# A ring of weight units made six deep instead of five, fetched five ahead, in a one-core decoder layer

## The chip, the cores and the metric

The kernel runs on one core of one Trainium2 chip. Its time is the device time of the core in microseconds; before the change the median of 3 runs is 420.98 us (420.36 to 421.74). The engines are TensorE (PE, matrix products), VectorE (DVE), ScalarE (ACT), GpSimd (POOL) and SyncE (SP), which here issues nearly all loads.

## The reference: what is computed

One layer of a decoder on 256 tokens of width 1024, in float32:

```python
proj = x @ w_in                       # all queries, keys, values of three mixers
o_a, o_b, o_c = sparse_attention(...), dilated_attention(...), block_attention(...)
gates = sigmoid(x @ w_gate)           # 3 x 1024 columns
merged = gates[0]*(o_a @ w_br_a) + gates[1]*(o_b @ w_br_b) + gates[2]*(o_c @ w_br_c)
x = layer_norm(ALPHA * x + merged @ w_out)
h = square(relu(x @ w_up)) @ w_down   # 1024 -> 4096 -> 1024
ple = sigmoid(x @ w_ple_gate) * (p @ w_ple)
x = layer_norm(ALPHA * x + h + ple)
```

A table of relative-position biases (one column per head) is added to all attention logits.

## The kernel before

**Products in three parts.** Each float32 product is made of three products of a shorter float type: every factor is split into a high part (a cast) and a low part (what the cast lost), and `prod` (L184, the matmul is L189) adds high x high, high x low and low x high in PSUM. The input `x` is split once into `xh` and `xl`. The weights come from memory and have to be split as they come.

**The ring of weights.** The class `Weights` (L80) keeps a list of units, in the order in which the program will use them; a unit is up to 128 x 1024 numbers (512 KB). `_split` handles one: SP loads it into a tile of the ring `raw` (L103), ACT casts it into a tile `whi` of the ring `part` (L110 or L112), and DVE subtracts the cast from the raw tile into `wlo` (L119 or L123); for the first 58 units POOL does the last columns of that. A raw tile is free again when the cast and the subtraction have read it; `whi` and `wlo` when TensorE has used them. `get(i, ahead)` (L128) hands out unit i, and before that makes sure that the units up to i + `ahead` have had their `_split` written into the program. `ahead` is `AHEAD` unless a caller gives another number: the steps of the wide products (L642, L651), their ends (`min(AHEAD, ...)`, L662 and L1044).

**What sets the order.** Each engine runs its instructions in a fixed order. It is not the order of the code: a scheduler that goes through the program with a simulated timeline places each instruction (L1158), and what has been written earlier goes first among those that are ready in that simulation. So a number like `AHEAD` can move instructions anywhere. SP's queue holds all loads of weights, the tiles `T` of the bias table (L265), the loads of `xr` (below) and the stores of the result; one that waits holds up those behind it.

**The stages.** (1) Until 17 us: first loads, split of `x`, first products. (2) Until 188.7 us the mixed part: the attention of the three mixers, with the products for their queries, keys and values, the gates (`fill("g")`) and the second and third branch (`fill("c")`, L335 to L348) put in between. `V` is cleared out of PSUM by L399, the keys by L318. (3) The merges: `merge(p)` for p = 0 to 3 (L675) multiplies the first branch by its weights (`w_br_a`), then DVE adds the gate (two L688, from PSUM into `G`), adds the other branches (L689), ACT writes the high half of two merged rows (two L693) and DVE the low half (two L694) into the tile `store`. (4) The out projection: `outp.step(k)` for k = 0 to 3 and then `finish` multiply the merged rows by the eight units of `w_out`, here called w0 to w7 (merged row k with w_k, four groups of three products; in each step the eight products with the high half of the row come first, then the four with the low half). The parts of w0 to w3 lie in the ring, those of w4 to w7 in the tile `store`, so in the orders below a split of w4 to w7 reads `store<-raw`. (5) First layer norm, the small branch `ple` and its gate, until 247 us. (6) The up projection until 330.5 us: 32 units, each 16 matmuls (L918, L921). (7) The down projection until 412 us. Pairs of its units go through a Strassen scheme: SP loads a pair into `xr` (L871, L873), DVE forms sums of its blocks (`form`, L880 to L882), and four tiles are split instead of two. (8) The second layer norm and the output, until 418.6 us.

Of the kernel before, what the change touches and what calls it, by code (L numbers as in the profile page):

```python
# [35 lines left out]
AQ, AK, AV, IQ, IK, IW, BQ, BK, BV, CQ, CK, CV = (  # L36
    0, 384, 448, 512, 1024, 1088, 1096, 1864, 2120, 2376, 2760, 3144)

AHEAD = 4
FIRST = 4  # L40
DV = 640

# [37 lines left out]
class Weights:  # L80
# [46 lines left out]

    def get(self, i, ahead=AHEAD):  # L128
        while self.done <= min(i + ahead, len(self.units) - 1):
            with ExitStack() as held:  # L130
                held.enter_context(self.tc.high_priority(offset=self.units[self.done][6]))
                ins = self.after
                if self.units[self.done][2] is not None:

                    ins = (*ins, self.copies[-1], self.subs[-1])
                for x in ins:
                    held.enter_context(self.tc.issue_after(x))
                self._split(self.done)
            self.done += 1
        return self.parts.pop(i)  # L140
# [3 lines left out]
def hybrid_layer(ctx: ExitStack, tc: tile.TileContext, x0, xn, pT, wqk, wva, wvb, wg, wbc, wba,  # L144
                 wout, wup, wdn, wpg, wple, lnrow, rel, onehot, pick, out):
    nc = tc.nc
    pe, act, dve, pool = nc.tensor, nc.scalar, nc.vector, nc.gpsimd

    keep = ctx.enter_context(tc.tile_pool(name="keep", bufs=1))
    raw = ctx.enter_context(tc.tile_pool(name="raw", bufs=5))  # L150
    part = ctx.enter_context(tc.tile_pool(name="part", bufs=5))
    queries = ctx.enter_context(ExitStack())
    qpool = queries.enter_context(tc.tile_pool(name="q", bufs=8))
    dram = ctx.enter_context(tc.tile_pool(name="dr", bufs=1, space=DRAM))
# [479 lines left out]
    class Wide:  # L634
# [6 lines left out]

        def get(self, k, ahead=AHEAD):  # L642
            if k not in self.ws:
                self.ws[k] = W.get(self.units[k], ahead)
# [5 lines left out]

        def step(self, k, ahead=AHEAD, bs=(0, 1), last=None, whole=None):  # L651

            self.get(k, ahead)
            for b in bs:
                for c, cs in enumerate(H):
                    end = (whole or len(self.units)) if cs in self.cut[b] else last
                    self.go(self.acc[b][c], k, b, cs, 0, end - 1)

        def finish(self, ks, done, spare):

            for k in ks:
                self.ws[k] = W.get(self.units[k], min(AHEAD, ks[-1] - k + spare))  # L662
            for b in range(2):
# [379 lines left out]
    X = p2.tile([128, 2, D], F32, name="X", tag="X")  # L1043
    ws = {k: W.get(u_dn[k][0], min(AHEAD, 31 - k)) for k in LATE}  # L1044
    accs = (P[4], P[8]), (P[2], *ends)
# [116 lines left out]
```

## Time and profile before

| | us |
|---|---|
| median of 3 runs | 420.98 |
| profiled execution | 420.38 |
| span in the profile | 418.6 |
| TensorE busy | 405.4 (97%) |
| DVE busy | 350.7 (84%) |
| ACT busy | 277.4 (66%) |
| POOL busy | 120.5 (29%) |

The profile is of one execution; 1.8 us of it lie outside the span. The granted clock of TensorE is 0.996 of full speed. A wait that the profile lists as "A <- B" is time in which engine A stood still, and B is what ended it.

### The profile page before, as it was taken

What the parts mean: (1) busy time and instruction counts of PE and PEld (TensorE: products, weight loads), DVE (VectorE), ACT (ScalarE), POOL (GpSimd) and SP (SyncE); (2) the same over time, 40 slices, a digit from 0 to 9 for tenths busy, and PEclk for the clock granted to TensorE, in tenths of its full rate; (3) what the DMA queues carried; (4) which work ended last, traced back from release to release, by engine and by line L of the source; (5) the groups of instructions that cost most, each with busy time, mean ns of one, the idle gap of its engine ahead of it and who ended that gap; (6) DMA issues with size and microseconds to landing.
All of it is one profiled execution on the core that took longest, in us unless ns stands there. A gap on an engine that the chain in (4) does not pass through costs nothing.

```text
span 418.6 us, 7824 instructions
## 1 busy us (share of the span) xinstructions
PE 405.4 (97%) x2804; PEld 373.6 (89%) x2804; DVE 350.7 (84%) x650; ACT 277.4 (66%) x530; POOL 120.5 (29%) x128
## 2 busy tenths in 40 slices
PE   7999999999999999999999999999999999999993
PEld 7988999999999999999787889999999988788883
DVE  4969668978778679889977889999999788999856
ACT  5878366396798885866606567887789766467320
POOL 1579456254354558500000002432430000000001
PEclk9999999999999999999999999999999999999998
DMA  8795977567465407479790686786576277555602
GB/s 282 279 325 171 258 255 204 151 205 275 129 216 159 133 0 262 144 223 333 246 329 0 203 299 199 223 284 201 177 221 207 91 279 236 173 176 198 205 2 101
DMA packets 28300, 84.30 MB, mean 201 GB/s; under 512 B 2992, under 2 KB 7128, under 8 KB 27876
## 3 DMA queue, kind: packets, MB, share of 16 engines
q1 hardware_dynamic: 26880, 79.41, 58.7%
q10 hardware_dynamic: 1284, 4.32, 3.0%
q8 instruction: 22, 0.36, 0.4%
q14 instruction: 18, 0.15, 0.1%
q0 software_dynamic: 96, 0.06, 0.0%
HBM read 81.88 MB, written 1.90 MB: 200 GB/s over the span
## 4 chain that ended last, share of the span: by engine, by line
PE 66%; DVE 15%; DMA 10%; issue 4%; ACT 2%; POOL 1%; SPq 1%; DVEq 0%; ACTq 0%; POOLq 0%
PE mm L189 26%; PE mm L918 13%; PE b L189 12%; PE mm L921 7%; DVE wlo L119 6%; PE b L368 2%; DMA xr<-in_wdn_dram 2%; DMA raw<-in_wqk_dram 2%; DMA raw<-in_wout_dram 2%; PE b L514 2%; DVE wlo L123 2%; DMA G<-in_x_dram 1%; ACT whi L112 1%; PE b L410 1%; DMA raw<-in_wg_dram 1%
## 5 line engine op out<-in xcount | busy, mean ns | idle before, releaser
L112 ACT CAST whi<-raw 128x1024 fp32r<-128x1024 f32 (+3 forms) x92 | 89.7, 986 | 39.1 <-PE b L189 14.3
L123 DVE TENSOR_TENSOR wlo<-raw,whi 128x256 fp32r<-128x256 f32 (+3 forms) x118 | 96.7, 843 | 16.8 <-ACT whi L112 13.6
L189 PE MATMUL mm<-xh,whi 128*128 128x256 f32 x336 | 89.2, 278 | 0.0
L123 POOL TENSOR_TENSOR wlo<-raw,whi 128x384 fp32r<-128x384 f32 (+1 forms) x50 | 68.1, 1371 | 69.6 <-ACT whi L112 68.2
L189 PE MATMUL mm<-xl,whi 128*128 128x256 f32 x336 | 86.9, 276 | 0.0
L189 PE MATMUL mm<-xh,wlo 128*128 128x256 f32 x336 | 79.9, 279 | 1.3 <-DVE k L318 0.8
L189 PEld LDWEIGHTS mm<-xh,whi 128*128 128x128 f32 x336 | 64.4, 192 | 0.9
L189 PEld LDWEIGHTS mm<-xl,whi 128*128 128x128 f32 x336 | 64.5, 192 | 0.1
L918 PE MATMUL mm<-x,whi 128*128 128x512 f32 x256 | 60.7, 379 | 0.0
L189 PEld LDWEIGHTS mm<-xh,wlo 128*128 128x128 f32 x336 | 58.8, 192 | 2.1 <-PE mm L189 0.9
L189 PE MATMUL b<-whi,store 128*128 128x512 f32 x168 | 52.6, 380 | 1.0 <-DVE store L694 0.7
L918 PEld LDWEIGHTS mm<-x,whi 128*128 128x128 f32 x256 | 46.1, 190 | 5.2
L119 DVE TENSOR_TENSOR wlo<-raw,whi 128x1024 fp32r<-128x1024 f32 (+2 forms) x38 | 42.9, 1153 | 3.3 <-ACT whi L112 3.1
L735 POOL TENSOR_TENSOR rs<-rs,half 128x1 f32<-128x1 f32 x4 | 2.7, 664 | 142.2 <-DVE rs L734 142.2
L110 ACT CAST whi<-raw 128x256 fp32r<-128x256 f32 x64 | 36.4, 612 | 6.1 <-PE b L189 3.7
L189 PEld LDWEIGHTS b<-whi,store 128*128 128x128 f32 x168 | 31.7, 189 | 6.0 <-DVE store L694 1.1
L921 PEld LDWEIGHTS mm<-x,wlo 128*128 128x128 f32 x256 | 33.6, 191 | 1.7
L921 PE MATMUL mm<-x,wlo 128*128 128x256 f32 x256 | 33.7, 275 | 0.0
L189 PE MATMUL b<-wlo,store 128*128 128x512 f32 x84 | 32.1, 382 | 0.7 <-DVE wlo L119 0.6
L942 POOL TENSOR_TENSOR a<-a 128x128 f32<-128x128 f32 x7 | 7.3, 1044 | 58.4 <-ACT a L904 52.8
L189 PE MATMUL mm<-op,whi 128*128 128x256 f32 x128 | 22.1, 278 | 0.0
L189 PE MATMUL b<-whi,x 128*128 128x512 f32 x64 | 19.8, 384 | 0.1
(223 smaller groups left out, 822.5 us busy)
## 6 DMA issues: line engine op xcount, KB each, us to landing
raw<-in_wup_dram SPq DMA_DIRECT2D x32, 512.0 KB
raw<-in_wg_dram SPq DMA_DIRECT2D x24, 512.0 KB
raw<-in_wqk_dram SPq DMA_DIRECT2D x18, 512.0 KB
raw<-in_wdn_dram SPq DMA_DIRECT2D x18, 512.0 KB
raw<-in_wout_dram SPq DMA_DIRECT2D x8, 512.0 KB
raw<-in_wpg_dram SPq DMA_DIRECT2D x8, 512.0 KB
T<-tabd SPq DMA_DIRECT2D x24, 128.0 KB
xr<-in_wdn_dram SPq DMA_DIRECT2D x6, 512.0 KB
```

The lines of the kernel that those rows point to most:

```text
L110: i = nc.scalar.copy(blocks(hi, a, b), blocks(r, a, b))
L112: i = nc.scalar.copy(hi, r)
L119: i = e.tensor_tensor(lo[:, x], r[:, x], hi[:, x].bitcast(F32), op=ALU.subtract)
L123: i = e.tensor_tensor(blocks(lo, *x), blocks(r, *x), blocks(hi, *x).bitcast(F32), op=ALU.subtract)
L189: i = pe.matmul(ps, lhsT=a[x], rhs=b[y], start=first and n == 0, stop=last and n == 2, skip_group_check=more)
L368: m = pe.matmul(ss[2 * n + h][:, QC[b]], lhsT=q[d, x, c], rhs=k[d, y, 0:128 * (b + 1)], start=i == 0, stop=i == 2)
L410: pe.transpose(t[:, 128 * i:128 * i + 128], P[:, 128 * i:128 * i + 128], ident)
L514: pe.matmul(pairs(first[f]), lhsT=w[:, k, 128 * f:128 * f + 128], rhs=inturn(x[:, k]), start=k == i == 0, stop=k == KT - 1 and i == 2)
L735: pool.tensor_tensor(rs, rs, half, op=ALU.pow)
L918: pe.matmul(ps, lhsT=hi[:, c], rhs=x1[:, :, k].rearrange("p b a t -> p a t b"), start=k == 0, stop=False)
L921: pe.matmul(ps[:, 0], lhsT=lo[:, c], rhs=x1[:, :, k, 0].rearrange("p b t -> p t b"), start=False, stop=k == KT - 1)
L942: pool.tensor_tensor(sums[2], a11, a21, op=ALU.subtract)
```

## The change

`AHEAD` goes from 4 to 5, the rings `raw` and `part` get six tiles each instead of five, and the argument `dynamic_dma_scratch_size=2048` shrinks the memory that is set aside in SBUF for transfers whose descriptors are written by POOL. There are three such transfers, all at the start (the bias table's inputs, L479 to L481). The freed memory is 14336 bytes per partition, and the ring needs 13312 more (4096 for a `raw` tile, 4352 for `whi`, 4864 for `wlo`).

```diff
--- before.py
+++ after.py
@@ -36,7 +36,7 @@
 AQ, AK, AV, IQ, IK, IW, BQ, BK, BV, CQ, CK, CV = (
     0, 384, 448, 512, 1024, 1088, 1096, 1864, 2120, 2376, 2760, 3144)
 
-AHEAD = 4
+AHEAD = 5
 FIRST = 4
 DV = 640
 
@@ -147,8 +147,8 @@
     pe, act, dve, pool = nc.tensor, nc.scalar, nc.vector, nc.gpsimd
 
     keep = ctx.enter_context(tc.tile_pool(name="keep", bufs=1))
-    raw = ctx.enter_context(tc.tile_pool(name="raw", bufs=5))
-    part = ctx.enter_context(tc.tile_pool(name="part", bufs=5))
+    raw = ctx.enter_context(tc.tile_pool(name="raw", bufs=6))
+    part = ctx.enter_context(tc.tile_pool(name="part", bufs=6))
     queries = ctx.enter_context(ExitStack())
     qpool = queries.enter_context(tc.tile_pool(name="q", bufs=8))
     dram = ctx.enter_context(tc.tile_pool(name="dr", bufs=1, space=DRAM))
@@ -1149,7 +1149,8 @@
     from concourse.bass_utils import run_bass_kernel_spmd
 
     laid = _layout(**{n: np.asarray(a) for n, a in inputs.items()})
-    nc = bacc.Bacc("TRN2", target_bir_lowering=False, num_devices=1)
+    nc = bacc.Bacc("TRN2", target_bir_lowering=False, num_devices=1,
+                   dynamic_dma_scratch_size=2048)
     arrays, args = {}, []
     for n, a in laid.items():
         arrays[f"in_{n}_dram"] = a
```

No instruction is added or taken away. What moves is their order. Three places follow, each before and after; "x2" is a row that comes twice in a row.

DVE in the merges, from the split of w1 or w2 (`wlo<-raw,whi`, of the out projection) to the first or second pair of L694. Before:

```order
L119 TENSOR_TENSOR wlo<-raw,whi 128x1024
L689 TENSOR_TENSOR G<-G 128x2x256
L688 SCALAR_TENSOR_TENSOR G<-G,mm 128x256 x2
L119 TENSOR_TENSOR wlo<-raw,whi 128x1024
L688 SCALAR_TENSOR_TENSOR G<-G,mm 128x256 x2
L694 SCALAR_TENSOR_TENSOR store<-G,store 128x256
L689 TENSOR_TENSOR G<-G 128x2x256
L694 SCALAR_TENSOR_TENSOR store<-G,store 128x256
L119 TENSOR_TENSOR wlo<-raw,whi 128x1024
L688 SCALAR_TENSOR_TENSOR G<-G,mm 128x256 x2
L689 TENSOR_TENSOR G<-G 128x2x256
L119 TENSOR_TENSOR store<-raw,store 128x1024 x3
```

After:

```order
L119 TENSOR_TENSOR wlo<-raw,whi 128x1024
L348 TENSOR_TENSOR G<-G,mm 128x256
L689 TENSOR_TENSOR G<-G 128x2x256
L688 SCALAR_TENSOR_TENSOR G<-G,mm 128x256 x2
L119 TENSOR_TENSOR wlo<-raw,whi 128x1024
L119 TENSOR_TENSOR store<-raw,store 128x1024
L688 SCALAR_TENSOR_TENSOR G<-G,mm 128x256 x2
L689 TENSOR_TENSOR G<-G 128x2x256
L119 TENSOR_TENSOR store<-raw,store 128x1024 x2
L688 SCALAR_TENSOR_TENSOR G<-G,mm 128x256 x2
L694 SCALAR_TENSOR_TENSOR store<-G,store 128x256 x2
L119 TENSOR_TENSOR store<-raw,store 128x1024
```

Before, the first L694 follows the split of w2, and w3 and the first three store units come between it and the second pair. After, the split of w3 and those of w4, w5 and w6 are ahead of the first L694, and only one store unit is left behind it.

ACT at the same place, from the load of the residual `X` (L719, on ACT's queue) to the first pairs of L693. Before:

```order
L719 DMA X<-in_xn_dram 128x2048
L112 CAST whi<-raw 128x768
L112 CAST whi<-raw 128x1024 x3
L693 ACTIVATE store<-G 128x256 x2
L112 CAST whi<-raw 128x1024
L112 CAST store<-raw 128x1024 x3
L693 ACTIVATE store<-G 128x256 x2
L112 CAST store<-raw 128x1024
```

After:

```order
L719 DMA X<-in_xn_dram 128x2048
L112 CAST whi<-raw 128x1024 x4
L112 CAST store<-raw 128x1024 x3
L693 ACTIVATE store<-G 128x256 x2
L112 CAST store<-raw 128x1024
L112 CAST whi<-raw 128x1024
L693 ACTIVATE store<-G 128x256 x2
L112 CAST whi<-raw 128x1024
L693 ACTIVATE store<-G 128x256 x2
```

Before, the first pair of L693 follows three casts of 1024 columns (w0 to w2). After, it follows seven: w0 to w3, and w4 to w6 into `store`.

SP where the down projection begins, with its loads `raw` (single units) and `xr` (pairs). Before:

```order
L103 DMA raw<-in_wup_dram 128x1024 x12
L103 DMA raw<-in_wdn_dram 128x1024 x5
L871 DMA xr<-in_wdn_dram 128x1024
L873 DMA xr<-in_wdn_dram 128x512 x2
L871 DMA xr<-in_wdn_dram 128x1024
L873 DMA xr<-in_wdn_dram 128x512 x2
```

After:

```order
L103 DMA raw<-in_wup_dram 128x1024 x11
L103 DMA raw<-in_wdn_dram 128x1024 x7
L871 DMA xr<-in_wdn_dram 128x1024
L873 DMA xr<-in_wdn_dram 128x512 x2
L871 DMA xr<-in_wdn_dram 128x1024
L873 DMA xr<-in_wdn_dram 128x512 x2
```

Seven loads into the ring stand ahead of the first `xr` where five stood, and one follows the second pair where two did.

## The prediction

> **What bounds the kernel now.** I read the head of the page first, then TensorE's waits, then the same busy times by stretch.
>
> ```profile
> span 418.6 us, 7824 instructions
> PE 405.4 (97%) x2804; PEld 373.6 (89%) x2804; DVE 350.7 (84%) x650; ACT 277.4 (66%) x530; POOL 120.5 (29%) x128
> q0 software_dynamic: 96, 0.06, 0.0%
> PE b L180 <- POOL ident masks.py:199: 1.7, 1, 1.7
> PE mm L189 <- DVE k L318: 0.8, 1, 0.8
> PE b L514 <- ACT sh L507: 0.7, 1, 0.7
> PE b L189 <- DVE store L694: 0.7, 1, 0.7
> PE b L189 <- DVE wlo L119: 0.7, 2, 0.6
> PE mm L189 <- DVE V L399: 0.6, 1, 0.6
> PE mm L189 <- DVE wlo L123: 0.4, 1, 0.4
> PE b L189 <- DVE b L992: 0.3, 1, 0.3
> SPq L103 <- DVE wlo L123: 142.5, 72, 13.4
> SPq L265 <- DMA tabd<-tab: 9.0, 1, 9.0
> ```
>
> TensorE is the bound: 97% of the span, and its waits (in us: total, times, longest) add up to 5.9. A deeper ring can act on those for weights or for what stands behind a split: the two split rows (0.7 and 0.4), the V row (0.6), and perhaps the store row (0.7). That is 2.4 us, 0.6%, the most that can be won unless an order changes elsewhere. The large number, 142.5 us of SP waiting for a ring slot, is cover and not cost: SP issues nothing else that is due then.
>
> ```profile
> 80.00:188.70 108.70, 107.65 (x936) 104.60 (x935) 86.56 (x216) 82.57 (x186) 52.42 (x46) 1.00 0.56 175
> 188.70:212.00 23.30, 22.56 (x140) 20.44 (x140) 23.06 (x37) 14.87 (x20) 0.00 (x0) 1.00 0.84 287
> 247.00:330.50 83.50, 83.50 (x512) 76.68 (x511) 80.40 (x126) 70.04 (x149) 21.49 (x28) 1.00 0.66 204
> 330.50:412.00 81.50, 80.04 (x383) 68.56 (x381) 70.75 (x83) 41.46 (x47) 0.55 (x1) 1.00 0.54 179
> ```
>
> These are stretches (from:to, length; PE, PEld, DVE, ACT, POOL busy with counts; clock, DMA share, GB/s). One stretch stands out: from 188.7 to 212 (the merges and the out projection) DVE is busy 23.06 of 23.30 us. There DVE has no slack, so the order in which its work stands decides when TensorE may go on. In the up projection (247 to 330.5) TensorE is busy throughout and waits for nothing.
>
> **The change, part by part. The merges** carry the largest term. With one more unit allowed ahead, the splits of w3 and of the store units w4, w5, w6 now stand ahead of the merged rows on both DVE and ACT. What the trace of before has there (start, duration, engine, operation, idle and releaser):
>
> ```profile
> 188.75 0.95 DVE L123 TENSOR_TENSOR wlo<-raw,whi 128x768 fp32r<-128x768 f32 x1
> 195.13 1.22 DVE L119 TENSOR_TENSOR wlo<-raw,whi 128x1024 fp32r<-128x1024 f32 x1 [0.24 <-ACT whi L112]
> 196.27 0.74 DVE L688 SCALAR_TENSOR_TENSOR G<-G,mm 128x256 f32<-128x256 f32 x2
> 196.93 0.42 DVE L694 SCALAR_TENSOR_TENSOR store<-G,store 128x256 fp32r<-128x256 f32 x1
> 197.27 0.68 DVE L689 TENSOR_TENSOR G<-G 128x512 f32<-128x512 f32 x1
> 200.60 3.49 DVE L119 TENSOR_TENSOR store<-raw,store 128x1024 fp32r<-128x1024 f32 x3
> 204.01 0.75 DVE L694 SCALAR_TENSOR_TENSOR store<-G,store 128x256 fp32r<-128x256 f32 x2
> ```
> ```profile
> 195.00 0.71 ACT L693 ACTIVATE store<-G 128x256 fp32r<-128x256 f32 x2
> 197.76 1.04 ACT L112 CAST store<-raw 128x1024 fp32r<-128x1024 f32 x1 [0.16 <-DMA raw<-in_wout_dram]
> ```
> ```profile
> 196.67 0.38 PE L189 MATMUL b<-whi,store 128*128 128x512 f32 x1
> 198.40 1.24 PE L189 MATMUL b<-whi,store 128*128 128x512 f32 x5
> 204.48 1.35 PE L189 MATMUL b<-whi,store 128*128 128x512 f32 x5 [0.74 <-DVE store L694]
> ```
>
> Step 0 of the out projection starts at 196.67 with the high half of merged row 0 (L693). At 198.40 come its products with the low half, which DVE had started to write at 196.93 (L694). Start to start a split takes 1.14 us (195.13 to 196.27), a pair of L688 0.66 (196.27 to 196.93), an L689 0.60 (197.27 to 197.87, where the next L694 starts; by its record 0.68).
>
> In the changed order four splits (4 x 1.14 = 4.56), one L688 pair (0.66) and one L689 (0.60) move ahead of the first L694: 5.82 us. Against that, DVE enters the stretch one split richer (the 768-wide one at 188.75, 0.86 start to start), and the 0.24 us of idle time at 195.13 goes, since w2's load is issued a slot earlier. So L694 starts 5.82 - 0.86 - 0.24 = 4.72 us later, at 201.65, and its first row is there at 202.0. Step 0's low products start then instead of at 198.40: 3.6 us late.
>
> ACT is not what ends last. If the load of w6 takes the place in time that w5 had, its cast starts at 197.76, takes 1.04, and L693 follows at about 198.8. TensorE then starts step 0 near 199.2, does eight products until 200.9, and waits for DVE until 202.0. If w6's load came no earlier than before, about one cast later, the eight products would end at about 202.1, the same point within 0.1.
>
> Part of the lag comes back at once. Before, TensorE stood for 0.74 us at 204.48, because three splits were ahead of the second pair of L694 on DVE. After, step 2's low products are due at about 207.2, and the L694 that they need follows the first pair by two splits and an L689: 201.65 + 0.75 + 2 x 1.14 + 0.60 = 205.3. That stall is gone. Net 3.6 - 0.74 = **+2.9 us**. Upper end +4 (a cast or the wait for a load comes on top, 1.04, with a little more). Lower end +0.5, if DVE got two more splits (2.3 us) done before 188.7. What stands behind it, LN1's statistics and then the gates and the up projection, is late by the same amount, and by the row of 247 to 330.5 TensorE has no idle time there to make it up.
>
> **The mixed attention** (until 188.7) has weights at two stalls:
>
> ```profile
> 92.33 1.24 DVE L123 TENSOR_TENSOR wlo<-raw,whi 128x640 fp32r<-128x640 f32 x1 [0.31 <-ACT whi L112]
> 93.49 1.01 DVE L399 TENSOR_TENSOR V<-mm,V 128x384 fp32r<-128x384 f32 x2
> 94.09 0.38 PE L189 MATMUL mm<-xh,wlo 128*128 128x256 f32 x1 [0.56 <-DVE V L399]
> 156.34 0.49 PE L189 MATMUL mm<-op,wlo 128*128 128x256 f32 x2 [0.39 <-DVE wlo L123]
> ```
>
> At 94.09 TensorE waits for a PSUM bank that L399 clears, and L399 stands behind the split at 92.33. In the changed order a split more has been done by then, so L399 can start about 1.16 us sooner (92.33 to 93.49) and the whole 0.56 goes. At 156.34 the unit's own split is late by 0.39; with a unit more in stock it should not be. Together 0.95, and I take **-1.0**. The lower end is -2.0, twice that, for small gaps that the waits don't list. The upper end comes from SP: three more raw loads now stand ahead of the first bias tiles (T, L265), 512 KB each and 3.0 us at the 175 GB/s of the row of 80 to 188.7, 9.0 us in all. SP's queue already stands 9.0 us for the bias table at that place, which covers them; if half of one load sticks out, the bias tiles and the softmax behind them are 1.5 late, so +1.5.
>
> **The down projection** (330.5 to 412) is where DVE has to split the loaded weights and form the Strassen sums.
>
> ```profile
> 330.70 0.33 SPq L871 DMA_DIRECT2D xr<-in_wdn_dram  x1
> 333.27 1.23 DVE L119 TENSOR_TENSOR wlo<-raw,whi 128x1024 fp32r<-128x1024 f32 x1 [0.74 <-ACT whi L112]
> 335.62 1.23 DVE L880 TENSOR_TENSOR rows<-xr 128x1024 f32<-128x1024 f32 x1 [0.79 <-DMA xr<-in_wdn_dram]
> 337.30 1.23 DVE L119 TENSOR_TENSOR wlo<-xr,whi 128x1024 fp32r<-128x1024 f32 x1 [0.46 <-ACT whi L112]
> 340.22 0.81 PE L189 MATMUL b<-whi,PL 128*128 128x512 f32 x3
> 356.28 1.23 DVE L880 TENSOR_TENSOR Y<-xr 128x1024 f32<-128x1024 f32 x1 [1.58 <-DMA xr<-in_wdn_dram]
> ```
>
> DVE stands idle 0.74 + 0.79 + 0.46 + 1.58 = 3.57 us here for casts and loads, and TensorE waits for splits 0.7 us in all (the row of waits above, two times; 81.50 - 80.04 = 1.46 us of every kind). In the changed order the splits of units 2 and 3 come a turn earlier, inside the up projection, where DVE has 83.5 - 80.4 = 3.1 us to spare. That fills the idle 0.74 and perhaps some of the rest. Against it, the first xr load stands behind seven raw loads instead of five. It waits for the last reader of x1 until 330.70 in any case. The seventh raw load needs the slot that unit 2's split frees at about 330, so its 512 KB (2.9 us at 179 GB/s) may be on the queue when xr is issued. TensorE needs the first split of the pair at 340.22 and has it at 338.5, 1.7 us early; a delay of up to 1.7 is covered, 1.2 more is not. I take **-0.7**, the waits for splits, since the filled 0.74 is as large; the ends are -1.5 (all of TensorE's idle time) and +1.2.
>
> The Trainium skill speaks against this part ("DMA: Bandwidth & Descriptors", Queues, rings and completion order): on each DMA engine descriptors are consumed in ring order, so what SP issues first goes first. By that the whole seventh load would lie ahead of xr. No row of before shows seven loads ahead of it.
>
> **The rest at 0**: LN1 and the ple gate get one more cast between turns of ACT, which is busy 66%; ends -0.5 and +0.5. The shrunken memory for dynamic transfers serves q0 alone, with 96 packets and 0.06 MB; 0 unless its three transfers now wait for each other, which I bound by one landing of the longest of them, 5.6 us:
>
> ```profile
> DMA to landing us min/median/max: 5.6/5.6/5.6
> ```
>
> Only the bias table hangs on them, and that this decides is less than 1 in 20. The Trainium skill ("DMA: Bandwidth & Descriptors", Terms) says that such transfers have their 16-byte descriptors written to rings in SBUF. With one or two descriptors a packet, 96 packets would be 1.5 or 3 KB, an estimate on either side of the new size; no run here shows what it costs.
>
> **Sum**: +2.9 - 1.0 - 0.7 + 0 = +1.2 us. The profiled execution took 420.38 us (span 418.6 and 1.8 around it), 0.6 under the median of 420.98. 420.38 + 1.2 = 421.6; on the scale of the median **422.2**, a shade slower.
>
> **Rivals.** *Slower, the longer queue*: the merges cost the full 2.9, the mixed stage gains nothing as T comes late behind the three loads, and xr comes 1.2 later than its cover: 2.9 + 0 + 1.2 = +4.1, 425.1. For it: T and xr share SP's queue with the ring, and DVE waits for xr even now. Against it: the cover of 1.7 us. It decides from a delay of xr above 1.7 us. *Faster, the stock pays*: the mixed stage reaches its lower end (-2.0), the down stage -1.0, and in the merges DVE comes two splits richer, so that the lag shrinks to 0.5: -2.5, 418.5. For it: the waits exist, and DVE has idle time before 188.7 (86.56 busy of 108.70). Against it: four splits stand ahead of L694 and the merges have none. *Nothing*: the ring fills off TensorE's path and DVE comes in time everywhere, 421.0. For it: 97% busy. Against it: the new order on DVE in a stretch without slack.
>
> **How the numbers follow.** The forecast has 0.45, the slower rival 0.18, the faster one 0.22, nothing 0.15. No more than 0.3% (1.26 us) can be told from no change here. As 422.2 lies close to the upper edge of what is the same (422.24), I put of the forecast a tenth on faster, four tenths on the same and half on slower; of the slower rival all on slower; of the faster rival nine tenths on faster; of the last all on the same. That is faster 0.04 + 0.20 = 0.24, same 0.18 + 0.02 + 0.15 = 0.35, slower 0.23 + 0.18 = 0.41. The forecast's own range is 420.5 to 423.9 (1.7 to both sides, as the ends of its terms seldom fall together); with most of the two outer rivals 418.6 to 424.9.
>
> **What would show it.** In the profile of the change: the first L694 ends near 202 and not 197.3, TensorE has a wait for L694 or for L693 of 2.5 to 3.6 us near 199 to 202, and the stall at 204.48 is gone; the wait for L399 near 94 is gone; the first xr lands 0 to 1.5 us later against the end of the up projection. It is wrong if the first low products come within 1 us of the last merge product, or if DVE is idle in the merges.

## The result and the profile after

The changed kernel takes 424.78 us (median of 6 runs, 423.47 to 426.58), the kernel before 421.34 us (median of 6, 419.25 to 421.74): the ratio is 1.0102, with a 95% interval of 1.0078 to 1.0125. It is slower by 1%, which by the ratio is some 4.3 us; the two medians alone are 3.4 apart, and in the later series the kernel before had medians of 420.2 to 420.5. The profiled execution took 424.71 us, its span is 422.9, so 4.3 more than the span of before.

First the head of its page, then what TensorE waited for (in us: total, times, longest), then the stretches with the borders used before (length; busy time of TensorE, its weight loads, DVE, ACT and POOL).

```profile
span 422.9 us, 7823 instructions
PE 405.8 (96%) x2804; PEld 375.1 (89%) x2804; DVE 353.2 (84%) x650; ACT 277.3 (66%) x530; POOL 116.0 (27%) x128
```
```profile
PE b L189 <- DVE store L694: 2.9, 1, 2.9
PE b L189 <- DVE b L992: 1.9, 1, 1.9
PE mm L189 <- DVE k L318: 1.4, 2, 0.8
PE b L414 <- DVE pt L412: 0.7, 1, 0.7
PE mm L189 <- DVE wlo L119: 0.4, 1, 0.4
PE mm L189 <- DVE V L399: 0.4, 1, 0.4
PE b L189 <- ACT store L693: 0.3, 1, 0.3
PE b L368 <- DVE q L305: 0.3, 1, 0.3
```
```profile
80.00:188.70 108.70, 107.23 (x932) 104.00 (x932) 86.78 (x213) 83.03 (x186) 50.13 (x45) 1.00 0.54 172
188.70:212.00 23.30, 20.11 (x132) 18.27 (x132) 23.23 (x38) 14.88 (x21) 0.00 (x0) 1.00 0.89 309
330.50:412.00 81.50, 79.20 (x377) 68.85 (x376) 69.83 (x81) 43.27 (x52) 0.55 (x1) 1.00 0.52 168
```

The work is the same: TensorE is busy for 405.8 us, 0.4 more than before. What grew is its waits. Two are new in size: 2.9 us for the low half of the merged rows (it was 0.7), and 1.9 for a sum at the end of the down projection (it was 0.3). In the stretch of the merges TensorE fell from 22.56 to 20.11 us busy, while DVE stayed full, 23.23 of 23.30.

The last matmul of a stage says where the 4.3 us between these two traces arose. Against before, the last product of the merges ends 1.0 us later (197.8 against 196.8), that of the out projection 3.7 later (222.3 against 218.6), that of the up projection again 3.7 (334.4 against 330.7), and the last of all 4.3 (415.9 against 411.6). So the mixed part and the merge products gave 1.0, the out projection 2.7, the layer norm and the up projection nothing, and the down projection 0.6. The 1.0 and the 0.6 are no larger than what two executions of one order differ by (next section); the 2.7 is.

In the out projection it looks like this (start, duration, engine, operation, idle and releaser; DVE, ACT, then TensorE):

```profile
197.21 1.22 DVE L119 TENSOR_TENSOR store<-raw,store 128x1024 fp32r<-128x1024 f32 x1
199.61 2.36 DVE L119 TENSOR_TENSOR store<-raw,store 128x1024 fp32r<-128x1024 f32 x2
202.54 0.76 DVE L694 SCALAR_TENSOR_TENSOR store<-G,store 128x256 fp32r<-128x256 f32 x2
```
```profile
194.85 2.94 ACT L112 CAST store<-raw 128x1024 fp32r<-128x1024 f32 x3
197.69 0.72 ACT L693 ACTIVATE store<-G 128x256 fp32r<-128x256 f32 x2
```
```profile
198.16 0.48 PE L189 MATMUL b<-whi,store 128*128 128x512 f32 x1 [0.32 <-ACT store L693]
203.02 1.35 PE L189 MATMUL b<-whi,store 128*128 128x512 f32 x5 [2.87 <-DVE store L694]
```

The splits of w4, w5 and w6 (`store<-raw`) run before the first L694. TensorE has done its eight products with the high half by 200.2 and stands until 203.02.

At the end of the down projection DVE has four splits, then one, then two ahead of the sum L992 that TensorE needs; before it had three, one and two. Before:

```profile
383.01 3.49 DVE L119 TENSOR_TENSOR wlo<-raw,whi 128x1024 fp32r<-128x1024 f32 x3
387.74 1.22 DVE L119 TENSOR_TENSOR wlo<-raw,whi 128x1024 fp32r<-128x1024 f32 x1
390.07 2.35 DVE L119 TENSOR_TENSOR wlo<-raw,whi 128x1024 fp32r<-128x1024 f32 x2
392.35 0.69 DVE L992 TENSOR_TENSOR b<-b,Y 128x512 f32<-128x512 f32 x1
```

After, on DVE and then on TensorE:

```profile
386.30 4.63 DVE L119 TENSOR_TENSOR wlo<-raw,whi 128x1024 fp32r<-128x1024 f32 x4
391.45 1.22 DVE L119 TENSOR_TENSOR wlo<-raw,whi 128x1024 fp32r<-128x1024 f32 x1
393.78 2.36 DVE L119 TENSOR_TENSOR wlo<-raw,whi 128x1024 fp32r<-128x1024 f32 x2
396.65 0.70 DVE L992 TENSOR_TENSOR b<-b,Y 128x512 f32<-128x512 f32 x1
```
```profile
397.40 0.48 PE L189 MATMUL b<-whi,store 128*128 128x512 f32 x1 [1.92 <-DVE b L992]
```

### The profile page after: what moved, and what is told of

It is laid out like the page before. It is cut to its first block, busy times and chain, and to the rows that moved or that the text cites. A ratio compares the mean times of both kernels' runs of the same rounds, so it can differ in the third digit from the quotient of the medians.

```text
span 422.9 us, 7823 instructions
## 1 busy us (share of the span) xinstructions
PE 405.8 (96%) x2804; PEld 375.1 (89%) x2804; DVE 353.2 (84%) x650; ACT 277.3 (66%) x530; POOL 116.0 (27%) x128
## 4 chain that ended last, share of the span: by engine, by line
PE 74%; DVE 16%; issue 4%; DMA 3%; ACT 1%; DVEq 0%; POOL 0%; SPq 0%; POOLq 0%; ACTq 0%
PE mm L189 32%; PE mm L918 13%; PE b L189 13%; DVE wlo L119 7%; PE mm L921 7%; PE b L368 3%; PE b L514 3%; DMA xr<-in_wdn_dram 2%; DMA pr<-in_pT_dram 1%; DVE wlo L123 1%; PE b L410 1%; DVE rows L880 1%; DVE Y L880 1%; PE b L414 1%; DVE store L119 1%
## 5 line engine op out<-in xcount | busy, mean ns | idle before, releaser
L123 DVE TENSOR_TENSOR wlo<-raw,whi 128x256 fp32r<-128x256 f32 (+3 forms) x118 | 101.0, 882 | 13.1 <-ACT whi L112 9.4
L123 POOL TENSOR_TENSOR wlo<-raw,whi 128x384 fp32r<-128x384 f32 (+1 forms) x50 | 64.4, 1299 | 72.1 <-ACT whi L112 53.9
L189 PE MATMUL mm<-xh,wlo 128*128 128x256 f32 x336 | 80.3, 279 | 1.8 <-DVE k L318 1.4
L942 POOL TENSOR_TENSOR a<-a 128x128 f32<-128x128 f32 x7 | 6.3, 894 | 60.3 <-ACT a L904 50.0
```

Of the source, the lines that this page charges most:

```text
L123: i = e.tensor_tensor(blocks(lo, *x), blocks(r, *x), blocks(hi, *x).bitcast(F32), op=ALU.subtract)
L189: i = pe.matmul(ps, lhsT=a[x], rhs=b[y], start=first and n == 0, stop=last and n == 2, skip_group_check=more)
L942: pool.tensor_tensor(sums[2], a11, a21, op=ALU.subtract)
```

## The experiments

The theory at this point: the time went into the order of DVE's work, since a deeper ring lets splits that nobody needs yet run ahead of rows and sums that TensorE waits for. The rivals: the loads set the pace (the longer queue on SP), the shrunken memory costs by itself, or fetching five ahead costs and not the sixth tile. Each kernel below was timed against the kernel before on the same chip.

### The memory alone

```diff
-AHEAD = 5            raw, part: bufs=6
+AHEAD = 4            raw, part: bufs=5
```

(against the change, so that only `dynamic_dma_scratch_size=2048` is left of it)

> Edit: only the memory for dynamic transfers shrinks to 2048 bytes; ring of five, four ahead. Every engine's order is that of before. If the shrunken memory costs nothing (theory): the median of before, within 0.3 us. If the three transfers of POOL's queue wait for each other (rival): the bias table later than 38.3 us and up to 5 us longer.

419.92 us against 420.3, ratio 0.9998 (0.9978 to 1.0018). The memory costs nothing. The order of every engine is that of before, so this run is also a second execution of the same order: its span is 416.4 us where that of before is 418.6. So much a single trace can differ: 1.2 of these 2.2 us had arisen by the end of the merge products, 0.3 arose in the out projection and 0.7 in the down projection. The 1.0 us of the mixed part and the 0.6 of the down projection lie within that.

### The sixth tile alone

```diff
-AHEAD = 5
+AHEAD = 4
```

> Edit: ring of six tiles, but still four units ahead (with the small memory). In the merges the store units w4 to w6 still stand ahead of the first L694, and the down projection has the order of the change. Theory (the ring's depth moves the order, not AHEAD): the merges lose 2.5 to 4 us and the end of the down projection about 1.6, as in the change; the mixed part may differ. Time 423 to 426. Rival (fetching five ahead is what costs): back to 421 to 422.

426.98 us, ratio 1.0156 (1.0131 to 1.0182), even slower, and 1 us beyond the expected range. The depth of the ring moves the order: with a free tile the scheduler can place a split earlier, whether or not the code asks for it one unit sooner. The waits for L694 (2.3 us) and L992 (1.8 us) are both there:

```profile
PE b L189 <- DVE store L694: 2.3, 1, 2.3
PE b L189 <- DVE b L992: 1.8, 1, 1.8
PE mm L189 <- DVE wlo L123: 1.2, 1, 1.2
```

The third row belongs to the mixed part, where one split (L123) came late by 1.2 us; the same wait was 0.4 before and is gone in the change, so it looks like the price of four ahead in a ring of six, by one trace. Fetching five ahead is therefore not what costs.

### Merged rows ahead of the store units

```diff
                     ins = (*ins, self.copies[-1], self.subs[-1])
+                    if self.stores < 4:
+                        ins += self.rows[1 if self.stores < 2 else 2]
+                    self.stores += 1
...
-            act.mul(m[:, 0], g[:, f], 0.5)
+            i = act.mul(m[:, 0], g[:, f], 0.5)
...
+        W.rows.append((i.ins, j.ins))
```

> Edit: the change, with the splits of w4 and w5 placed behind the second pair of L693 and L694 and those of w6 and w7 behind the third. Everything outside the merges keeps the order of the change. Theory (the splits ahead of the first L694 cost 2.7 us): the low products of step 0 wait less than 0.5 us instead of 2.9, and the time falls by 2.7 to 3.7 to about 421.5. Rival (the loads of the store units set the pace): the wait turns into one for a load or a cast, and the time falls by less than 1.

420.07 us, ratio 0.9996 (0.9974 to 1.0018): all of the loss is gone, 4.5 to 4.7 us against the change by the ratios and the medians, more than the 3.7 at which the expectation ended. The first L694 (its line is 698 here) starts at 197.63 and TensorE goes from the merges into the out projection without a wait. DVE in this kernel:

```profile
197.63 0.42 DVE L698 SCALAR_TENSOR_TENSOR store<-G,store 128x256 fp32r<-128x256 f32 x1
201.31 0.76 DVE L698 SCALAR_TENSOR_TENSOR store<-G,store 128x256 fp32r<-128x256 f32 x2
202.58 2.36 DVE L120 TENSOR_TENSOR store<-raw,store 128x1024 fp32r<-128x1024 f32 x2
```

In the trace the last product of the out projection ends at 218.3, 4.0 us before that of the change and 0.3 before that of the kernel before: the new waits of 0.32 and 2.87 are gone, and also the old one of 0.74, which the change had removed anyway. The loads of `w_out` are issued in the same order on SP as in the change and each 0.2 us sooner, as the merges too end 0.2 us sooner, so they did not set the pace there.

That more came back than the waits themselves has a likely reason in the other traces: a wait here can cost more than its length. Three kernels were traced with the wait for the low rows in place: the change, the run with the sixth tile alone (2.3 us), and the run with the late sums first, further below (2.6 us). In the last two TensorE's granted clock is halved for over 3 us from 0.5 and 1.0 us behind the wait's end; in the profiled execution of the change it is not. The stretch from 200 to 210 us of the change, of the sixth tile alone and of the late sums first, then the halved part in the run with the sixth tile alone (the clock is the third number from the end):

```profile
200.00:210.00 10.00, 7.13 (x33) 6.16 (x33) 10.00 (x16) 5.01 (x10) 0.00 (x0) 1.00 0.89 277
200.00:210.00 10.00, 7.37 (x25) 5.83 (x26) 10.00 (x16) 5.29 (x8) 0.00 (x0) 0.83 0.90 287
200.00:210.00 10.00, 7.79 (x28) 6.53 (x29) 10.00 (x18) 4.83 (x9) 0.00 (x0) 0.83 0.87 283
```
```profile
205.20:208.50 3.30, 3.30 (x9) 2.63 (x8) 3.30 (x6) 1.28 (x2) 0.00 (x0) 0.50 0.91 300
```

A mean of 0.83 over 10 us is 1.7 us of TensorE's work lost. From the last merge product to the last of the out projection it takes 24.4 us in the trace of the change, 25.7 and 26.1 in these two, and 20.7 here. The mean clock of the change's runs is 0.997 in the profiled one and 0.988 to 0.993 in the other five (0.994 to 0.998 in those of the kernel before); one such stretch is worth 0.004 of the mean, so most of them probably had it too. They were not traced, and their times do not follow the clock closely, so this part of the 4.7 us is not settled.

### The same placing in the kernel before

The same lines in the kernel before.

> Edit: the kernel before (ring of five, four ahead, large memory), with the same placing of w4 to w7 behind the second and third pair. Theory: the 0.74 us wait of TensorE for L694 at 204.48 goes, 0.7 to 1.0 us faster than before, about 420.4. Rival (w4 to w7 then come late for the end of the out projection): no gain or up to 1 us slower.

420.29 us, ratio 0.9999 (0.9979 to 1.0018): nothing won. In the out projection the gain came: its last product ends 21.02 us after the last of the merges where that of before took 21.73. It was lost at once behind it, in the layer norm. TensorE waits for L748 (the normalised rows), and DVE itself for the layer norm's scale and shift, whose load ACT's queue issued only at 212.89, behind casts that waited for weights (before: 209.30). The waits of TensorE and of DVE:

```profile
PE b L774 <- DVE Y L748: 1.6, 1, 1.6
DVE Y L744 <- DMA rows<-in_lnrow_dram: 2.4, 1, 2.4
```

### Sums ahead of the last units

The first lines let the program fetch no further ahead than unit 25, the last ones place the units 26 to 29 behind a sum.

```diff
...
+        if k in ((20, 21), 22, 23):
+            W.ahead = 4 if k == (20, 21) else 25 - k
...
-    plus(P[8], P[8], v35)
+    p8_made = plus(P[8], P[8], v35)
...
+    W.after = (p8_made,)
     ws = {k: W.get(u_dn[k][0], min(AHEAD, 31 - k)) for k in LATE}
+    W.after = ()
```

> Edit: the change, but the splits of the units 26 to 29 of the down projection are placed behind the sums that complete two of its accumulators (the second and third L992 into PSUM); the merges stay as in the change. Theory (at the end of the down projection TensorE waits 1.9 us because these splits stand ahead of the sums on DVE): that wait falls under 0.5, 1.4 to 2.2 us faster than the change, about 422.9. Rival (the late loads of pairs, 1.9 us behind those of before, set this wait): the wait moves to a split and less than 0.7 is won.

422.54 us, ratio 1.0051 (1.0033 to 1.0069), half of the loss gone (2.1 to 2.2 us by the ratios and the medians). TensorE's waits for L992 and for splits have left the list. From the end of the up projection to the last matmul it takes 78.5 us, against 81.5 in the change and 81.0 before. In this trace 1.7 us of that gain are lost in the out projection by the halved clock shown above.

### Both placings, and the share of POOL

> Edit: the change with both placings, the merged rows ahead of w4 to w7 and the sums ahead of the units 26 to 29. Theory: the two waits are in different stages, so their gains add: 1.1 to 1.6 us under the run with the rows alone (420.07), about 418.7, and faster than the kernel before. Rival (the end is bound by the splits of the last units anyway): the same as with the rows alone.

417.95 us, ratio 0.9935 (0.9917 to 0.9952), faster than the kernel before by 2.5 us and 0.8 under the time expected. The gains add. The order of the end, in which one split is ahead of the sums (L1001 here) and four follow them:

```profile
383.63 1.22 DVE L121 TENSOR_TENSOR wlo<-raw,whi 128x1024 fp32r<-128x1024 f32 x1
384.76 0.68 DVE L1001 TENSOR_TENSOR Y<-mm,Y 128x512 f32<-128x512 f32 x1
387.29 0.69 DVE L1001 TENSOR_TENSOR b<-b,Y 128x512 f32<-128x512 f32 x1
388.49 4.62 DVE L121 TENSOR_TENSOR wlo<-raw,whi 128x1024 fp32r<-128x1024 f32 x4
```

and the stretch of the down projection (its length, then the busy time of TensorE, its weight loads, DVE, ACT and POOL):

```profile
329.84:408.40 78.56, 78.48 (x381) 69.03 (x380) 69.04 (x81) 39.84 (x46) 0.55 (x1) 1.00 0.55 181
```

TensorE is busy 78.48 of 78.56 us, so in this trace nothing is left to win there by order.

TensorE waits for `k` (L318) near 29.6 us in the change. To see what makes this `k` late, the next kernel takes POOL's share of two units away. (It comes from the fourth L318 on DVE; the expectation calls it the third `k`.)

```diff
-        return W.add(*a, by=by if i < 58 else "v", at=at)
+        return W.add(*a, by=by if i < 58 and i not in (8, 9) else "v", at=at)
```

> Edit: as the run with both placings, and the low parts of the ninth and tenth unit are made wholly on DVE, so that POOL has no share of them. In the change a DVE split of 640 columns takes 2.03 us at 25.45 while POOL works through five splits without a pause, and TensorE waits 0.53 for the third k (L318) at 29.62. Theory (DVE and POOL hold each other up): the splits at that place take 1.3 us in all with their POOL part, the k comes 0.5 us sooner, the wait near 29.6 shrinks under 0.2 us. On the whole time 0.3 to 0.6, which a comparison hardly tells. Rival (the k is late because one more split stands ahead of it): the wait stays.

417.7 us, ratio 0.9931 (0.9908 to 0.9955), no difference to the run before it. The split at that place fell to 1.53 us with its POOL part instead of 2.03, but the `k` came at 28.77 where in the change it came at 29.04, and TensorE's two waits for `k`, at 29.35 and 40.14, were 1.6 us in all. The wait stays, so POOL is not all of its cause. A single trace says little here: in the run before this one, with POOL's share in place, the wait near 29.6 was absent.

### Where the layer norm's rows are loaded

```diff
-        act.dma_start(t, lnrow[i:i + 2] ...
+        (act if i else nc.sync).dma_start(t, lnrow[i:i + 2] ...
```

This is put on the kernel before with its merged rows first.

> Edit: the kernel before with the merged rows first (the fourth run), and the load of the layer norm's rows moved from ACT's queue, where it stood behind casts that wait for weights and was issued at 212.9, to SP's, behind the fourth unit of the gate. Theory (the 0.7 us won in the merges were lost again because DVE waited 2.4 us for these rows): issued near 209, the wait goes, and the time is 0.7 to 2 us under the kernel before and under the fourth run. Rival (the two loads share the same engines and land late in either queue): DVE still waits over 1 us for the rows and the time stays.

419.45 us, ratio 0.9975 (0.996 to 0.999): 0.8 us under the fourth run and 1.0 under the kernel before. The load is issued at 209.71 on SP, DVE no longer waits for it, and TensorE's wait for L748 is gone. So that was where the 0.7 us had been lost: from the last product of the out projection to the last of the up projection it took 112.1 us before, 114.8 in the fourth run and 112.1 here.

### Both rings with all placings

The kernel before with all three placings, then the ring of six with all three.

> Edit: the kernel before (ring of five, four ahead, large memory) with all three placings: merged rows first, sums first, the layer norm's rows on SP's queue. Theory (with the orders mended, a sixth tile is worth the waits for splits in the down projection, 1.85 us in the trace of before, which a ring of five keeps): 0.5 us under the eighth run, about 418.9, and 1 us or so above the ring of six with its placings (417.95). Rival (the placings are all there is, the ring's depth is worth nothing): the same as the ring of six, 418.

> Edit: the ring of six with all three placings; on SP the layer norm's rows stand behind six units of the gate, since the sixth tile lets two more of them in front. Theory (the place in the queue decides when they are issued, not which queue it is): issued near 211 as with ACT's queue, the wait for x near 224 (0.5 us) stays, the time is that of the run with two placings, 417.9, within 0.5. Rival (SP's queue frees them from ACT's casts): issued near 209, 0.5 to 0.7 us less.

418.65 us with five tiles (ratio 0.9961, 0.9944 to 0.9978) and 417.47 with six (0.993, 0.9903 to 0.9958). The sixth tile looks worth about 1.2 us once the orders are mended, but the two intervals overlap, so it is likely and not certain. In the traces it is the down projection: the ring of five still waits for splits, the ring of six does not; from the last up product to the last of all 80.1 against 78.5 us. The waits of the ring of five:

```profile
PE b L195 <- DVE wlo L121: 0.6, 1, 0.6
PE mm L195 <- DVE wlo L125: 0.4, 1, 0.4
```

The edit of the tenth kernel also gives the load of the layer norm's rows a higher priority for the scheduler. The rows were issued at 209.22, not near 211, so in that place SP's queue did free them from ACT's casts and the first part of that expectation is wrong. What that is worth on the time (0.5 us under the sixth run) can't be told.

## Why the prediction was wrong

It forecast +1.2 us, too near to no change to be told from it; the time rose by 1%, some 4.3 us. 424.78 lies above the range of the forecast itself (420.5 to 423.9), and inside the wider one only because the rivals stretch that. Of the sum the +2.9 came; the step that failed is the set-off against it, -1.0 in the mixed part and -0.7 in the down projection. Waits were crossed off because the stock of weights would be longer, and the waits that the new order makes in the same stages (for `k`, `q` and L992, below) were put at nothing. In their place the traces show +1.0 and +0.6, which is no gain, and no more than the scatter of single traces.

**The merges (+2.9): right in mechanism, and in size for the profiled execution.** The trace shows 2.7: the last product of the out projection went from +1.0 to +3.7. The first L694 was to start at 201.65 and started at 202.54; the lag of 1.0 from the stages ahead accounts for that. TensorE was to wait for DVE and not for ACT, as it did (2.87 against 0.32 us), though ACT had finished its casts 1.1 us sooner than forecast. The store units' loads landed early and were no limit. The third run, which changes the order there alone, confirms the place. In the two other traces with this wait the stage took 4.0 and 4.4 us more than before, 1.7 of it by the halved clock; the prediction has no term for that.

**The mixed part (-1.0): no gain was seen, and the size is not settled.** The wait at 156.34 went as forecast, and that for L399 shrank only from 0.56 to 0.38; in the other execution of the order of before it is absent. Three others came: 0.53 for a `k` (L318), 0.29 for a `q` (L305) and 0.71 for `pt` (L412). That for `k` near 29.6 us is in no trace with a ring of five and in five of the six with six tiles and five ahead (0.4 to 1.2 us); that for `q` near 164 us is in none of the former and in all of the latter (0.3). Together they undo what the two forecast waits gave. Over all traces the first product of the second branch ends at 138.4 to 139.6 us in five executions with a ring of five and at 139.1 to 140.6 in six with a ring of six and five ahead, 0.8 apart on average with the two spreads overlapping. The step that failed here is the one that took a list of waits for what a longer stock would remove, and did not ask what else is behind the splits that then run sooner. The bias tiles were covered, as forecast: SP's wait for the table fell from 9.0 to 1.7 us, as loads took its place, and the first tile was issued at 38.51 instead of 38.34. The profile does put waits of DVE down to a tile T in the change. But the instruction that waits is a split, which reads no T, and the same idle time stands in the trace of before with another releaser (before, then the change):

```profile
43.79 1.67 DVE L123 TENSOR_TENSOR wlo<-raw,whi 128x640 fp32r<-128x640 f32 x1 [1.51 <-ACT whi L112]
44.49 1.68 DVE L123 TENSOR_TENSOR wlo<-raw,whi 128x640 fp32r<-128x640 f32 x1 [1.52 <-DMA T<-tabd]
```

The `pt` wait came from a load: ACT waited 4.06 us for the load that L576 casts, 3.14 before, and `pt` stood behind that cast. Over all twelve traces the time from the end of this load's issue to its cast was 4.0 to 5.5 us with five tiles and 4.4 to 5.9 with six, and a wait for `pt` at the same place, of 0.2 us, stands in the second trace of the order of before, so its lateness isn't put down to the change. TensorE's wait for the `k`, ACT's cast of that load, then the wait of SP's queue for the bias table, all of the change:

```profile
29.62 0.35 PE L189 MATMUL mm<-xh,wlo 128*128 128x256 f32 x1 [0.53 <-DVE k L318]
```
```profile
99.78 0.62 ACT L576 CAST ph<-pr 128x512 fp32r<-128x512 f32 x1 [4.06 <-DMA pr<-in_pT_dram]
```
```profile
SPq L265 <- DMA tabd<-tab: 1.7, 1, 1.7
```

**The down projection (-0.7): no gain was seen, by a term that was left out.** What was said of its beginning holds: the xr load stood behind seven loads and DVE waited 4.31 us for it instead of 0.79. From the end of the up projection the first sum started 6.8 us later where before it was 4.95, so 1.9 us late against a cover of 1.7; TensorE lost 0.39 us there, at the third split of the pair and not at the first. The load was not issued late: SP issued it 0.03 us after the last up product in both traces (330.70 and 334.42), so the 1.9 us arose between issue and landing.

```profile
341.22 1.23 DVE L880 TENSOR_TENSOR rows<-xr 128x1024 f32<-128x1024 f32 x1 [4.31 <-DMA xr<-in_wdn_dram]
348.37 0.48 PE L189 MATMUL mm<-wlo,PL 128*128 128x512 f32 x1 [0.39 <-DVE wlo L119]
```

The waits for splits in this stage fell from 0.7 us to that one of 0.4, as forecast in kind. But the step looked at the weights' waits alone and passed over L992, which stood in the list of before with 0.3 us. It became 1.9: counted from the end of the up projection TensorE came to that place 1.1 us sooner than before, and the sum started 0.6 us later (62.3 against 61.7), with one split of 1.1 us more ahead of it, which is the same mechanism that the prediction had worked out in the merges. The fifth run, which mends that place alone, gave 2.1 us back. The whole stage took 80.3 to 81.4 us in four traces with five tiles and the order of before at its end, and 80.1 to 81.5 in three with six, so it came out even; with the sums first the ring of six needs 78.5, a gain larger than the one forecast. Of the skill's rule in this part (the Trainium skill, "DMA: Bandwidth & Descriptors", Queues, rings and completion order) the trace agrees: with seven loads ahead instead of five xr landed 1.9 us later, where a whole load had been put at 2.9.

**The memory and the rest (0): right.** The first run shows 0.9998, and the layer norm and the up projection kept the lag at 3.7 us to within 0.1. The Trainium skill ("DMA: Bandwidth & Descriptors", Terms) speaks of descriptor rings in SBUF; that a smaller one would hold up the three transfers is not seen.

**The rivals.** "The longer queue" named a time near the one measured, 425.1, for another reason: xr was 1.9 us late, more than the 1.7 from which that rival was to decide, but of its 1.2 us only 0.39 showed. "The stock pays" was, with its 2.5 us, what a ring of six gives once two places are mended by hand, 417.95; the change did not bring it about.

## What to carry to other kernels

Where a scheduler orders in-order engines, a deeper ring is a change of order: it can let work that is not yet due run ahead of work that is waited for, here at two places where DVE worked without a pause. Look in the new order for the short instructions on which the bound engine waits (here L694 and L992, 0.4 and 0.7 us each) and count what has moved ahead of them, at all such places and not at the most conspicuous one; then pin them. Set a gain against a loss only where the new order has been gone through for new waits too. A gain in one stage shows only if the next stage's inputs, here a load behind casts on ACT's queue, are early enough to use it.

## What the runs showed of the hardware

DVE and POOL slow one another when both work on weights. From 20 to 29 us DVE's split of 640 columns took 1029 ns in the mean before and 1464 ns after, when POOL ran five splits of 384 columns without a pause and was itself faster (1552 to 1333 ns). The means of single traces scatter: 864 to 1039 ns in three with five tiles, 1392 to 1467 in five with six. Groups of that stretch, of before, then of the change:

```profile
L123 DVE TENSOR_TENSOR wlo<-raw,whi 128x640 fp32r<-128x640 f32 x4 | 4.1, 1029 | 1.3 <-ACT whi L112 1.3
L123 POOL TENSOR_TENSOR wlo<-raw,whi 128x384 fp32r<-128x384 f32 x4 | 6.1, 1552 | 0.4 <-ACT whi L112 0.4
```
```profile
L123 DVE TENSOR_TENSOR wlo<-raw,whi 128x640 fp32r<-128x640 f32 x5 | 7.2, 1464 | 0.0
L123 POOL TENSOR_TENSOR wlo<-raw,whi 128x384 fp32r<-128x384 f32 x5 | 6.6, 1333 | 0.1
```

The Trainium skill ("SBUF — State Buffer", Who interferes with whom) says that a DVE instruction with two inputs in SBUF contends with a GpSimd one that reads SBUF. These rows agree, and the seventh run shows that taking POOL's share of two units away does not bring the stage forward: DVE then does the work itself.

TensorE's granted clock can halve for over 3 us behind a wait, which takes 1.7 us on top of the wait. It did so behind waits of 2.3 and 2.6 us and, near 30 us in the trace of the ring of six with all placings, behind one of 1.1 us (mean 0.66 from 30 to 35 us); it did not behind the 2.87 us in the change's profiled execution. What decides between the two is not shown.

Two executions of one order differed by 2.2 us in span (418.6 and 416.4), 1.2 of it by the end of the merge products. A term under 1 us there can't be read from one trace.
